# Two feed-forwards whose work is ordered by a planner or written out unit by unit, on one Trainium2 core

## The chip, the core and the metric

The kernel runs on one core of one Trainium2 chip. A core has five engines that run beside each other, each with its own queue of instructions: TensorE (PE, matrix products into the accumulator memory PSUM), VectorE (DVE), ScalarE (ACT), GpSimd (POOL) and SyncE (SP, which here only issues transfers). PE's loads of the stationary operand are listed apart (PEld). Each engine takes its instructions in order; an instruction that needs another engine's result waits on a semaphore. The metric is the device time of one execution in microseconds, and the kernel before is timed as the median of three runs.

## What is computed

A block of two layers over 512 positions `x` and 256 context positions, width 1024, all in float32. Each layer has a mixer (attention and others, not touched here) and a gated feed-forward whose input is normalised, scaled and shifted by modulation vectors; the modulation comes from a matrix `ada_w` times a small vector. The part that matters:

```python
def swiglu(h, w_in, w_out):
    g, u = jnp.split(h @ w_in, 2, axis=-1)
    return (jax.nn.silu(g) * u) @ w_out

    # per layer l
    mod = silu_c @ ada_w[l] + ada_b[l]
    modc = silu_cc @ ada_w[l] + ada_b[l]
    ...
    h = h + g2 * swiglu(modulate(h, norm2_g[l], sh2, sc2), ffn_w_in[l], ffn_w_out[l])
    if need_ctx:                       # layer 0 alone
        hc = hc + cg2 * swiglu(modulate(hc, norm2_g[l], csh2, csc2), ffn_w_in[l], ffn_w_out[l])
```

The hidden width is 2816, that is 22 hidden tiles of 128. Layer 0 works on 768 columns (positions and context), layer 1 on 512.

## The kernel before

**Products in three matmuls.** Every float32 operand is split in a high and a low part (`hi`, a rounded copy; `lo`, the rest). A product takes three matmuls per 128 rows: hi·hi, hi·lo, lo·hi (`mm3`, lines 100 to 102 of the profile). So each weight needs a cast on ScalarE (`slot`, line 913) and a subtraction on GpSimd or VectorE (line 917) before TensorE can use it.

**Seven products per hidden tile.** For hidden tiles 2 or 3 and up, the input product of a hidden tile is done by a scheme of seven half-size products instead of eight (`product`, numbered 1 to 7). Each has four steps of 128 rows: 12 matmuls of 384 columns in layer 0, of 256 in layer 1. The weights of products 1, 2 and 4 are quarters of the raw weight tile (`raw`, 1 MB, line 804); those of 5, 6, 3 and 7 are sums or differences that VectorE makes (line 968), all in one tile per hidden tile (`t` or `sq`). The results go to a wide PSUM tile of two banks, `pw`: products 1, 6, 7, 4 add up in its first half (`ps0`), 5 and 3 in its second (`ps1`); product 2 has a PSUM tile of its own. Between the products the partial sums are read out:

- after 1: copy of 2 (996), add (997), SiLU (999); after 6: copy (1001); after 5: copy into `u` (1005)
- after 3: add (1008), SiLU (1010); after 7: add to `u` (1012), multiplication (1014); after 4: multiplication (1017)
- then the hidden tile is split into hi and lo (116, 117)

**Output units.** The output product of a pair of hidden tiles is spread over later hidden tiles: per hidden tile four units a, b, c, d (`s2`), each for 128 output rows: 6 matmuls of 512 columns and, in layer 0, 6 of 256 for the context, into PSUM tiles `pb` of which there are three. VectorE adds each to the residual (766). Their weights come in tiles of 512 KB (`rawo`, line 925).

**Modulation of layer 1.** During layer 0's feed-forward, 48 tiles of `ada_w` are loaded on SyncE's queue (216) into two buffers and reduced by VectorE (222, "dots"); the first 16 of them serve positions and context, two dots each.

**Who sets the order.** The program is written in the order of lines 1079 to 1094, one string per hidden tile ("2156ab37cd4" and so on). Outside of a few explicit edges (`issue_after`), a planner then orders each engine's instructions by readiness and written order on an estimated timeline; so what stands in the queues is a mix of two or three hidden tiles. Waits are set per tile of memory, PSUM tiles included.

The loops in question are those over hidden tiles 3 to 21 in `ffn(0)` and `ffn(1)`. Ahead of them stand the direct tiles (two in layer 0, three in layer 1) and, in layer 0, hidden tile 2.

Of the kernel before, what the change touches and what calls it, by code (L numbers as in the profile page):

```python
# [6 lines left out]
F32 = mybir.dt.float32  # L7
# [7 lines left out]
P = 128  # L15
# [11 lines left out]
class Builder:  # L27
# [191 lines left out]
    def ada_dot(self, l, j, k, t, who):  # L219
        junk = self.adap.tile([P, D], BF16, name=self.uid("junk"), tag="junk", bufs=1)  # L220
        col = l * 48 + j * KT + k
        self.nc.vector.scalar_tensor_tensor(junk, t, 1.0, self.cb[who], ALU.mult, ALU.mult,
                                            accum_out=self.acc[who][:, col:col + 1])

# [538 lines left out]
    def residual(self, l, j, m, off, n, ps):  # L763
        for who, c, r in self.cols(off, n):
            h = self.h(who, m)[:, c]
            self.nc.vector.scalar_tensor_tensor(h, ps[:, r], self.modcol(l, j, m, who), h, ALU.mult, ALU.add)  # L766

# [34 lines left out]
    def ffn_in(self, l, f, pool):  # L802
        t = pool.tile([P, 2048], F32, name=self.uid("raw"), tag="raw", bufs=1 if pool is not self.Rf else 2)
        self.nc.sync.dma_start(t, self.a["ffn_in"][l, f])
        return t
# [43 lines left out]
    def ffn(self, l):  # L849
# [7 lines left out]
        if both:  # L857

            for n, shape, bufs in (("rawo", [P, 1024], 1), ("hs", [P, T], 1), ("u", [P, NH], 1), ("w", [P, 1024], 5)):
# [4 lines left out]
        def ada_some(n):  # L864
            for _ in range(min(n, len(todo))):
                ll, j, k = todo.pop(0)
                t = self.ada_tile(ll, j, k)
                for who in range(2 if j < 2 else 1):
                    self.ada_dot(ll, j, k, t, who)
# [39 lines left out]

        def slot(src, t=None):  # L910
            t = wtile() if t is None else t
            with tc.issue_after(self.first_sq.ins) if (3, 8)[l] <= self.nslot < 12 else ExitStack():
                nc.scalar.copy(t[:, 0, :], src)  # L913
            self.nslot += 1
            sums_due = (8, 12)[l] < self.nslot <= (15, 21)[l]
            eng = nc.vector if sums_due or l == 1 and self.nslot % 4 == 0 else nc.gpsimd
            eng.tensor_tensor(t[:, 1, :], src, t[:, 0, :].bitcast(F32), ALU.subtract)  # L917
            return t
# [3 lines left out]

        def load(src, cols):
            t = ring.tile([P, cols], F32, name=self.uid("rawo"), tag="rawo", bufs=(1, 2)[l])
            nc.sync.dma_start(t, src)
            return t

# [42 lines left out]

        def more(n, f, ins):

            if todo and n in (1, 3, 6, 7) and f >= 4:
                with tc.issue_after(ins.ins):
                    ada_some(1)

        def product(n, f):
# [16 lines left out]
            if n == 1:  # L994
                g = st["g"] = self.gated_tile(ring if f % 3 == 2 else None)
                nc.scalar.copy(g[:, :NH], st["p2"])
                ins = nc.vector.tensor_tensor(g[:, :NH], g[:, :NH], ps0, ALU.add)
                more(1, f, ins)
                nc.scalar.activation(g[:, :NH], g[:, :NH], AF.Silu)
# [6 lines left out]
            elif n == 3:  # L1006
                g = st["g"]
                ins = nc.vector.tensor_tensor(g[:, NH:], g[:, NH:], ps1, ALU.add)  # L1008
                more(3, f, ins)
                nc.scalar.activation(g[:, NH:], g[:, NH:], AF.Silu)  # L1010
            elif n == 7:
                ins = nc.vector.tensor_tensor(st["u"], st["u"], ps0, ALU.add)  # L1012
                more(7, f, ins)
                nc.vector.tensor_tensor(st["g"][:, NH:], st["g"][:, NH:], st["u"], ALU.mult)
            elif n == 4:
# [9 lines left out]
                del state[f], raws[f], sums[f]  # L1025
                more(4, f, self.last_s1)

        def s2_part(fs, m, W, off, n):
            ps = self.bank()[:, :n]
            self.dense(ps, W, [(hi[:, off:off + n], lo[:, off:off + n]) for hi, lo in [hid[f] for f in fs]])  # L1030
            self.residual(l, 5, m, off, n, ps)

        def s2_weights(g, m):

            if m % 4 == 0:
                outs[g] = load(a["ffn_out"][l, g, :, 256 * m:256 * m + 1024], 1024)
                if g == NF // 2 - 1:
                    f = NF + m // 4
                    pool = ring if l and f % 3 == 2 else self.Rf
                    self.big = pool.tile([P, 2048], F32R, name=self.uid("raw"), tag="raw", bufs=1 if pool is ring else 2)  # L1040
            if m % 2 == 0:
                o = m % 4 * 512
                t = self.big[:, o:o + 1024].rearrange("p (a b) -> p a b", a=2) if g == NF // 2 - 1 else None
                w2[g] = slot(outs[g][:, m % 4 * 256:m % 4 * 256 + 512], t)
            w = w2[g]
            return [(w[:, 0, c:c + P], w[:, 1, c:c + P]) for c in range(m % 2 * 256, m % 2 * 256 + 256, P)]

        def s2(g, m):

            W = s2_weights(g, m)  # L1050
            for off, n in whos:
                s2_part((2 * g, 2 * g + 1), m, W, off, n)

        hid, outs, w2, Wl = [], {}, {}, []

# [16 lines left out]
        for v in ("5 6 22 12 52 62 32 7 72 4 h 42", "5 6 d 4 7 h")[l].split():  # L1072
            if v == "d":
                direct(2, 1)
            elif v == "h":
                for f in range(nd):
                    hide(f)
            elif len(v) == 1:
                quarter(int(v))
            else:  # L1080
                product(int(v[0]), int(v[1]))
        for f in range(3, NF):
            todo_m = [(0, m) for m in range(8)] if f == 3 else [(f // 2 - 1, f % 2 * 4 + m) for m in range(4)]
            for v in ("2156ab37cd4", "2a1b56c3d74", "2a1b56c3de7f4ghij", "2a1b56c3de7f4g")[f % 2 if f < NF - 1 else l + 2]:
                if v in "abcd":
                    for _ in range(2 if f == 3 else 1):
                        s2(*todo_m.pop(0))
                elif v.isdigit():
                    product(int(v), f)
                else:  # L1090
                    m = "efghijkl".index(v)
                    Wl.append(s2_weights(NF // 2 - 1, m))
                    for off, n in whos:
                        s2_part((NF - 2,), m, Wl[m][:1], off, n)
        ahead = len(Wl)
        for m in range(ahead, KT):
            Wl.append(s2_weights(NF // 2 - 1, m))
        sq = self.sumsq()
# [305 lines left out]
```

## Time and profile before

| | us |
|---|---|
| median of three runs | 1640.68 |
| lowest, highest | 1636.35, 1644.80 |
| profiled execution, first to last instruction | 1641.9 |
| PE busy | 1542.8 |
| DVE busy | 1073.0 |
| POOL busy | 766.9 |
| ACT busy | 724.5 |

The profiled execution's own time is its span. A line of the groups reads: line of the kernel, engine, operation, output tile <- input tiles, shapes, count; then busy time in us and the mean of one in ns; then the idle time of the engine just before them and who ended it. A line of the timeline reads: start, duration, engine, line, operation; in brackets the idle time before it and its releaser. TensorE's matmuls are pipelined, so the durations of neighbours overlap, and the distance between starts tells the rate. A line of the busy time by windows reads: window, its length, then busy time and count of PE, PEld, DVE, ACT, POOL, the granted clock, the share of DMA time and GB/s. A line of the waits reads: who waited for whom, us in total, times, the longest.

### The profile page before, as it was taken

To read this page: it belongs to the slowest core of one execution; us is meant where nothing else is said; L and a number is where in the kernel's file an instruction comes from. 1 tells how busy PE (TensorE), PEld (TensorE's weight loads), DVE (VectorE), ACT (ScalarE), POOL (GpSimd) and SP (SyncE) were. 2 spreads that over 40 slices of the span, in tenths; PEclk is the share of its full clock that TensorE was granted. 3 is DMA by queue.
4 is the path that set the end of the run, shared out by engine and by line. 5 is a ranking of instruction groups with operands and counts; after the bars stand their busy time and mean duration, and the time that the engine had idled before them with its cause. 6 is when DMAs were issued, how large, how long until landed. Compare 5 with 4: busy or idle time off the path is not lost.

```text
span 1641.9 us, 24642 instructions
## 1 busy us (share of the span) xinstructions
PE 1542.8 (94%) x9547; PEld 1367.1 (83%) x9547; DVE 1073.0 (65%) x1980; ACT 724.5 (44%) x1472; POOL 766.9 (47%) x543
## 2 busy tenths in 40 slices
PE   6999989999999999999999988999989999999996
PEld 4776877899899889998989978777868989898886
DVE  4621788756857788666665585665667857666665
ACT  2423675645533233333333244555664544444443
POOL 0463221062157666666666316532222466675662
PEclk9999989999999999999999999999999999999998
DMA  8744100141223343343432012110233222322201
GB/s 317 298 153 169 40 7 1 65 139 68 76 79 116 105 139 131 105 150 126 142 131 77 27 51 91 52 33 25 74 116 123 65 103 92 101 90 103 90 27 52
DMA packets 47957, 161.98 MB, mean 99 GB/s; under 512 B 5472, under 2 KB 9952, under 8 KB 40160
## 3 DMA queue, kind: packets, MB, share of 16 engines
q1 hardware_dynamic: 47696, 160.28, 28.4%
q8 instruction: 75, 1.23, 0.3%
q14 instruction: 42, 0.34, 0.1%
q10 hardware_dynamic: 144, 0.13, 0.0%
HBM read 158.29 MB, written 2.10 MB: 98 GB/s over the span
## 4 chain that ended last, share of the span: by engine, by line
PE 69%; DVE 11%; POOL 6%; DMA 5%; ACT 4%; issue 3%; POOLq 0%; SPq 0%; DVEq 0%; ACTq 0%
PE pw L100 9%; PE pw L101 9%; PE pw L102 9%; PE pb L100 7%; PE pb L101 7%; PE pb L102 7%; POOL w L917 5%; DMA raw<-ffn_in 3%; PE pf L100 3%; PE pf L101 2%; PE pf L102 2%; PE pb L1257 2%; PE pb L1246 2%; PE pf L351 2%; DVE t L968 2%
## 5 line engine op out<-in xcount | busy, mean ns | idle before, releaser
L100 PE MATMUL pw<-ax,w 128*128 128x384 f32 (+2 forms) x732 | 237.5, 328 | 16.1 <-DVE q L1012 6.7
L101 PE MATMUL pw<-ax,w 128*128 128x384 f32 (+2 forms) x732 | 237.9, 325 | 4.1 <-DVE ax L458 2.5
L78 POOL TENSOR_TENSOR w<-raw,w 128x512 fp32r<-128x512 f32 (+1 forms) x84 | 127.6, 1526 | 243.2 <-ACT w L75 220.8
L102 PE MATMUL pw<-ax,w 128*128 128x384 f32 (+2 forms) x732 | 236.7, 325 | 2.1 <-POOL w L917 2.1
L917 POOL TENSOR_TENSOR w<-raw,w 128x512 fp32r<-128x512 f32 x119 | 177.7, 1507 | 54.2 <-ACT w L913 53.4
L917 POOL TENSOR_TENSOR w<-t,w 128x512 fp32r<-128x512 f32 x90 | 133.4, 1482 | 139.9 <-ACT w L913 136.5
L100 PE MATMUL pb<-hh,w 128*128 128x512 f32 x480 | 167.3, 362 | 12.8 <-ACT hh L116 8.3
L766 DVE SCALAR_TENSOR_TENSOR xT<-pb,mod,xT 128x512 f32<-128x512 f32 (+3 forms) x208 | 144.5, 704 | 43.8 <-PE pb L102 43.1
L101 PE MATMUL pb<-hh,w 128*128 128x512 f32 x480 | 171.2, 358 | 0.5 <-POOL hh L117 0.5
L102 PE MATMUL pb<-hh,w 128*128 128x512 f32 x480 | 170.7, 357 | 0.0
L100 PEld LDWEIGHTS pw<-ax,w 128*128 128x128 f32 x732 | 142.0, 195 | 27.2 <-DVE q L1012 8.1
L100 PE MATMUL pw<-T,w 128*128 128x384 f32 (+1 forms) x508 | 159.1, 314 | 4.8 <-DVE hs L1008 2.4
L101 PE MATMUL pw<-T,w 128*128 128x384 f32 (+1 forms) x508 | 158.6, 312 | 4.0 <-DVE T L117 4.0
L102 PE MATMUL pw<-T,w 128*128 128x384 f32 (+1 forms) x508 | 158.2, 312 | 0.0
L101 PEld LDWEIGHTS pw<-ax,w 128*128 128x128 f32 x732 | 142.6, 195 | 12.1 <-DVE ax L458 3.4
L102 PEld LDWEIGHTS pw<-ax,w 128*128 128x128 f32 x732 | 142.4, 195 | 6.0 <-POOL w L917 2.7
L913 ACT CAST w<-t 128x512 fp32r<-128x512 f32 x104 | 64.5, 621 | 176.8 <-DVE t L968 122.5
L917 POOL TENSOR_TENSOR w<-rawo,w 128x512 fp32r<-128x512 f32 x63 | 94.1, 1493 | 66.5 <-ACT w L913 66.5
L100 PEld LDWEIGHTS pb<-hh,w 128*128 128x128 f32 x480 | 89.5, 189 | 27.0 <-ACT hh L116 10.8
L100 PEld LDWEIGHTS pw<-T,w 128*128 128x128 f32 x508 | 97.2, 192 | 9.7 <-DVE hs L1008 3.9
L101 PEld LDWEIGHTS pw<-T,w 128*128 128x128 f32 x508 | 97.4, 192 | 6.6 <-DVE T L117 4.6
L102 PEld LDWEIGHTS pb<-hh,w 128*128 128x128 f32 x480 | 90.3, 188 | 13.1
(363 smaller groups left out, 4056.7 us busy)
## 6 DMA issues: line engine op xcount, KB each, us to landing
raw<-ffn_in SPq DMA_DIRECT2D x44, 1024.0 KB, 4.9
ar<-ada SPq DMA_DIRECT2D x24, 1024.0 KB, 7.3
ar<-ada SPq DMA_DIRECT2D x48, 512.0 KB, 3.5
rawo<-ffn_out SPq DMA_DIRECT2D x44, 512.0 KB, 3.9
raw<-odd_out SPq DMA_DIRECT2D x32, 256.0 KB, 2.7
raw<-qk SPq DMA_DIRECT2D x16, 256.0 KB, 7.9
raw<-uv SPq DMA_DIRECT2D x16, 256.0 KB, 2.7
raw<-even_out SPq DMA_DIRECT2D x8, 512.0 KB, 4.2
```

Of the source, the lines that this page charges most:

```text
L78: eng.tensor_tensor(lo, raw, hi.bitcast(F32), ALU.subtract)
L100: mm(out, s[0], m[0], start=start, stop=False, **kw)
L101: mm(out, s[0], m[1], start=False, stop=False, **kw)
L102: return mm(out, s[1], m[0], start=False, stop=stop, **kw)
L351: nc.tensor.matmul(ps[32 * q:32 * q + 32, :w], cst[:, k, :], t[:, w * q:w * q + w], start=k == 0, stop=k == KT - 1, skip_group_check=True)
L766: self.nc.vector.scalar_tensor_tensor(h, ps[:, r], self.modcol(l, j, m, who), h, ALU.mult, ALU.add)
L913: nc.scalar.copy(t[:, 0, :], src)
L917: eng.tensor_tensor(t[:, 1, :], src, t[:, 0, :].bitcast(F32), ALU.subtract)
L968: nc.vector.tensor_tensor(t, x, y, how)
L1246: last = nc.tensor.transpose(pt[:, x * P:(x + 1) * P], es[2 * (x % 2) + x // 2][:, kb * P:(kb + 1) * P], self.ident)
L1257: nc.tensor.matmul(po[64 * h:64 * h + 64, :], V[vb][:, 64 * g:64 * g + 64], t[:, h * TC:h * TC + TC], start=kb == 0, stop=kb == nb - 1, sk ...
```

## The change

It rewrites the loop over hidden tiles 3 to 21 of both feed-forwards.

- `run(key, ...)` issues an instruction after the last one that went through `run` with the same engine key, so that PE, DVE, ACT, POOL and SP each keep the written order within the loop.
- The loop is flattened into units: products and output units, per hidden tile 2 1 5 a 6 b 3 7 c d 4 for all of them.
- A second list, `jobs`, holds the weight preparations (sum where there is one, cast, low part) in the order of their use. Before the loop `R` jobs are issued, 8 in layer 0 and 12 in layer 1, and then one after each product and each pair of output units.
- Sums go to tiles of their own, three in turn, instead of one tile per hidden tile. Low parts go to GpSimd, in layer 1 those of output weights to VectorE.
- Output weights are loaded in half tiles (256 KB), two buffers in layer 0 and six in layer 1. Raw weights are loaded two or three hidden tiles ahead.
- Modulation tiles are loaded on ScalarE's queue, after 2, after 5 and after an output unit c, and reduced after 1, 3 and 4: three per hidden tile instead of four.
- Product 2 goes to the PSUM tile `pf` instead of one of the three `pb`.

```diff
+        def run(key, fn, *args, **kw):
+
+            with tc.issue_after(tail[key].ins) if key in tail else ExitStack():
+                tail[key] = fn(*args, **kw)
+            return tail[key]
...
+        def ada_load():
+            if todo:
...
+                run("ACT", nc.scalar.dma_start, t, a["ada1"][r:r + P, :])
+                tiles.append((ll, j, k, t))
...
+        nrawo = (2, 6)[l]
+        halves = [(g, h) for g in range(NF // 2) for h in range(4)]
+
+        def load():
+            if halves:
+                g, h = halves.pop(0)
+                t = ring.tile([P, 512], F32, name=self.uid("rawo"), tag="rawo", bufs=nrawo)
+                run("SP", nc.sync.dma_start, t, a["ffn_out"][l, g, :, h * 512:h * 512 + 512])
+                outs.append(t)
...
-            for v in ("2156ab37cd4", "2a1b56c3d74", "2a1b56c3de7f4ghij", "2a1b56c3de7f4g")[f % 2 if f < NF - 1 else l + 2]:
+            for v in "215a6b37cd4" if f < NF - 1 else ("215a6b37cdef4ghij", "215a6b37cdef4g")[l]:
...
+        R = (8, 12)[l]
...
+        def sum_tile():
+            self.ns += 1
+            sumt.append(self.sumsq()[:, :512] if self.ns % 3 == 2 else self.tmp("t"))
+            return sumt[-1]
...
+        def job():
...
+            if j[0] == "s":
+                Wt[j] = slot(outs.pop(0), None, ("POOL", "DVE")[l])
+                load()
...
+                    add("DVE", src, x, y, how)
+                Wt[j] = slot(src, None, "POOL")
...
+        def unit(n, f):
...
+            for j in range(4):
+                c = slice(j * P, (j + 1) * P)
+                run("PE", self.mm3, out, (w[:, 0, c], w[:, 1, c]), op[n][j], j == 0 and n in (1, 2, 5), j == 3)
...
+            if n == 2:
+                run("ACT", nc.scalar.copy, A, out)
+                ada_load()
+            elif n == 1:
+                add("DVE", A, A, ps0, ALU.add)
+                run("ACT", nc.scalar.activation, A, A, AF.Silu)
+                ada_dots()
+            elif n == 6:
+                run("ACT", nc.scalar.copy, B, ps0)
+            elif n == 5:
...
+                run("ACT", nc.scalar.copy, st["u"], ps1)
+                ada_load()
+            elif n == 3:
+                add("DVE", B, B, ps1, ALU.add)
+                run("ACT", nc.scalar.activation, B, B, AF.Silu)
+                ada_dots()
+            elif n == 7:
+                add("DVE", st["u"], st["u"], ps0, ALU.add)
+                add("DVE", B, B, st["u"], ALU.mult)
...
+        for _ in range(R):
+            job()
+        for u in units:
+            if u[0] == "s":
+                g, m = u[1:]
+                for off, n in whos:
+                    s2_part((2 * g, 2 * g + 1), m, pieces(Wt[("s", g, m // 2 * 2)], m), off, n, True)
+                if m % 4 == 2:
+                    ada_load()
+                if m % 2 == 0:
+                    continue
...
+            else:
+                unit(*u)
+            job()
```

More of the change, by code (lines that the diff above doesn't have):

```diff
@@ L1025, in product, with s2_part, pieces @@
                 del state[f], raws[f], sums[f]
-                more(4, f, self.last_s1)
-        def s2_part(fs, m, W, off, n):
+        def s2_part(fs, m, W, off, n, chain=False):
             ps = self.bank()[:, :n]
[L1030 to L1045, printed above, removed]
-            return [(w[:, 0, c:c + P], w[:, 1, c:c + P]) for c in range(m % 2 * 256, m % 2 * 256 + 256, P)]
[L1048 to L1054, printed above, removed]
+            A = [(hi[:, off:off + n], lo[:, off:off + n]) for hi, lo in [hid[f] for f in fs]]
+            if not chain:
+                self.dense(ps, W, A)
+                self.residual(l, 5, m, off, n, ps)
+                return
+            for k in range(len(W)):
+                run("PE", self.mm3, ps, W[k], A[k], k == 0, k == len(W) - 1)
+            run("DVE", self.residual, l, 5, m, off, n, ps)
+        def pieces(w, m):
+            return [(w[:, 0, c:c + P], w[:, 1, c:c + P]) for c in range(m % 2 * 256, m % 2 * 256 + 256, P)]
+        hid, outs = [], []
         nd = (2, 3)[l]
@@ L1086, in ffn @@
                     for _ in range(2 if f == 3 else 1):
[L1087 to L1097 removed]
+                        g, m = todo_m.pop(0)
@@ L1098, in ffn @@
+        ahead = sum(u[0] == "t" for u in units)
+        while jobs:
+            job()
         sq = self.sumsq()
```

121 lines of the change are left out of this document (98 added, 23 removed).

## The prediction

> **What bounds the kernel now.** I read the page's first part, then the busy time of the two feed-forward loops by windows, then single instructions in the timeline, then the lists of waits and the groups by shape.
>
> ```profile
> span 1641.9 us, 24642 instructions
> ...
> PE 1542.8 (94%) x9547; PEld 1367.1 (83%) x9547; DVE 1073.0 (65%) x1980; ACT 724.5 (44%) x1472; POOL 766.9 (47%) x543
> ```
>
> TensorE is busy 94% of the span. Busy is not full rate, so I take the rate from start times. First the loop of layer 0 (hidden tiles 3 to 21), then the same loop of layer 1:
>
> ```profile
> 470.00:930.00 460.00, 444.10 (x2486) 416.41 (x2485) 315.61 (x459) 156.57 (x282) 297.37 (x191) 0.99 0.34 115
> 1310.00:1610.00 300.00, 286.29 (x1929) 263.54 (x1927) 190.90 (x271) 126.95 (x262) 191.13 (x136) 0.99 0.25 85
> ```
>
> ```profile
> 663.08 0.33 PE L100 MATMUL pw<-ax,w 128*128 128x384 f32 x1
> ...
> 665.51 0.33 PE L102 MATMUL pw<-T,w 128*128 128x384 f32 x1
> ...
> 665.88 0.56 DVE L1012 TENSOR_TENSOR q<-q,pw 128x384 f32<-128x384 f32 x1 [0.47 <-PE pw L102]
> ...
> 666.39 0.39 PE L100 MATMUL pb<-hh,w 128*128 128x512 f32 x1
> ...
> 667.80 0.28 PE L100 MATMUL pb<-hh,w 128*128 128x256 f32 x1
> ...
> 668.39 0.28 PE L102 MATMUL pb<-hh,w 128*128 128x256 f32 x1
> ```
>
> ```profile
> 1608.68 0.28 PE L100 MATMUL pw<-ax,w 128*128 128x256 f32 x1
> ...
> 1609.64 0.28 PE L102 MATMUL pw<-ax,w 128*128 128x256 f32 x1
> 1610.03 0.42 DVE L1008 TENSOR_TENSOR hs<-hs,pw 128x256 f32<-128x256 f32 x1 [0.78 <-PE pw L102]
> ...
> 1610.50 0.39 PE L100 MATMUL pw<-T,w 128*128 128x256 f32 x1 [0.58 <-DVE hs L1008]
> 1610.73 0.28 PE L101 MATMUL pw<-T,w 128*128 128x256 f32 x1
> ```
>
> Undisturbed, a matmul of 384 columns follows the last after 0.174 us (14 steps from 663.08 to 665.51), of 512 after 0.235 (six from 666.39), of 256 after 0.12. A hidden tile of layer 0 has 84, 24 and 24 of them: 23.05 us, 0.175 each; one of layer 1 has 84 of 256 and 24 of 512: 15.7 us, 0.146 each. So the 2486 and 1929 matmuls of the windows need 434 and 281 us, and lose 26 and 19. **The change can win at most about 45 us in the loops**: the order that the planner found already overlaps two hidden tiles and is within 6% of TensorE's rate. The losses hang on late weights:
>
> ```profile
> PE pb L100 <- ACT hh L116: 8.3, 6, 2.9
> ...
> DVE t L968 <- DMA raw<-ffn_in: 19.2, 8, 5.2
> ...
> SPq L216 <- DVE junk L222: 246.9, 45, 15.0
> ```
>
> SyncE's queue stands 246.9 us behind the two modulation buffers, so raw weights come late, VectorE's sums wait 19.2 us for them, and TensorE waits at the end of that chain.
>
> **The change, part by part.**
>
> Weights 8 or 12 tiles ahead, sums in three tiles in turn, output weights in 256 KB halves, modulation loads on ScalarE's queue: these remove that chain. Raw weights are asked for two or three hidden tiles ahead, a half tile two tiles of work before its use, and 8 tiles are some 20 us. So I credit all 45 us. The halves cost 44 more issues on SyncE, and 48 issues move to ScalarE, which is busy 156.57 of 460 us; if their cover goes, one half tile costs its landing:
>
> ```profile
> raw<-odd_out SPq DMA_DIRECT2D x32, 256.0 KB, 2.7
> ```
>
> ```profile
> L917 POOL TENSOR_TENSOR w<-raw,w 128x512 fp32r<-128x512 f32 x55 | 86.1, 1573 | 15.7 <-ACT w L913 14.9 <-DVE t L968 0.8
> ...
> L117 POOL TENSOR_TENSOR hh<-hs,hh 128x768 fp32r<-128x768 f32 x19 | 36.4, 1917 | 5.3 <-ACT hh L116 5.1
> ```
>
> All low parts of layer 0 go to GpSimd (9 per tile of 1.57 us and one of 1.92: 16 of at least 23 us) and cost nothing while it stays below TensorE's time. A modulation load on ScalarE waits for the dot two loads back (two buffers); behind it stand the cast of a weight 8 tiles ahead and an activation that waits for VectorE anyway: 0, or one dot of 1.54 us if that cover goes. VectorE and ScalarE get 129 and 119 more semaphore instructions; they are short and lie in the queues walked through below.
>
> The written order of TensorE is the part that costs. Each hidden tile is 2 1 5 a 6 b 3 7 c d 4, chained. Products 1, 6, 7, 4 fill one half of a wide PSUM tile and 5, 3 the other, but the program waits for the tile, not the half: in the row at 1610.50 product 7 (first half) waits for VectorE's add of product 3 (second half). In the new order product 5 stands right behind 1 and 7 right behind 3, with nothing between, and the compiled program has exactly these waits. Before, the planner put other work there, and few such waits show (layer 1: us in total, times, longest):
>
> ```profile
> PE pw L100 <- DVE hs L1008: 1.8, 3, 0.8
> ```
>
> I call each place a join. Its least price: in layer 1, 1609.64 to 1610.50 is 0.86 us instead of 0.12, and the second matmul comes 0.11 late: 0.85. In layer 0, VectorE starts 0.37 after the last matmul's start (665.51 to 665.88) and takes 0.56; with the same rest that is 0.37 + 0.56 + 0.05 − 0.17 + 0.11 = 0.92. Two joins, 19 tiles, two layers: 19 × 2 × (0.92 + 0.85) = 67 us. **Joins alone eat the 45 and 22 more.**
>
> VectorE's order is chained too, so an add behind a join waits for whatever was written before it. Layer 1:
>
> ```profile
> L766 DVE SCALAR_TENSOR_TENSOR xT<-pb,mod,xT 128x512 f32<-128x512 f32 x69 | 50.3, 742 | 1.0 <-PE pb L102 0.9
> L968 DVE TENSOR_TENSOR t<-raw,t 128x512 f32<-128x512 f32 x11 | 17.3, 1569 | 3.2 <-POOL w L917 3.2
> L917 DVE TENSOR_TENSOR w<-rawo,w 128x512 fp32r<-128x512 f32 x12 | 15.8, 1320 | 4.1 <-ACT w L913 3.8
> L968 DVE TENSOR_TENSOR t<-raw 128x512 f32<-128x512 f32 x21 | 14.7, 699 | 35.7 <-DMA raw<-ffn_in 19.9 <-POOL w L917 15.8
> ```
>
> ```profile
> L913 ACT CAST w<-rawo 128x512 fp32r<-128x512 f32 x33 | 20.4, 620 | 0.0
> ...
> L996 ACT COPY hs<-pb 128x256 f32<-128x256 f32 x17 | 6.3, 370 | 2.7 <-PE pb L102 2.7
> ```
>
> ```profile
> L917 POOL TENSOR_TENSOR w<-raw,w 128x512 fp32r<-128x512 f32 x43 | 61.5, 1446 | 11.8 <-ACT w L913 11.8
> ...
> L117 POOL TENSOR_TENSOR hh<-hs,hh 128x512 fp32r<-128x512 f32 x18 | 28.7, 1595 | 0.4 <-ACT hh L116 0.3
> ```
>
> A product takes TensorE 1.43, an output unit 1.4. From the end of product 2 at 0: ScalarE has copied it out (0.37) at 0.95, since the cast of a sum stands ahead to 0.55, casts (0.62) an output half tile to 1.6, VectorE makes its low part (1.32) to 2.95, and only then adds product 1, to 3.35. Product 5 begins at 3.45; product 1 had ended at 1.43. Wait with the slow second matmul: 2.1. At the other join the residual of b (0.74) and another low part stand before the add of product 3: 5, a, 6 and b follow each other from 3.45 to 9.2, residual to 10.1, low part to 11.45, add to 11.9; product 3 ended at 10.6: 1.4. Together 3.5 us. A VectorE instruction of this size takes 0.70 where GpSimd leaves it alone (the row of t<-raw); with that for the low parts it is 1.55 + 0.85 = 2.4. Layer 1: 46 to 66 us.
>
> Layer 0, with modulation dots behind products 1, 3 and 4:
>
> ```profile
> L222 DVE SCALAR_TENSOR_TENSOR junk<-ar,cb 128x1024 bf16<-128x1024 f32 x64 | 98.6, 1541 | 0.2
> L766 DVE SCALAR_TENSOR_TENSOR xT<-pb,mod,xT 128x512 f32<-128x512 f32 x77 | 57.3, 744 | 20.2 <-PE pb L102 20.1
> ...
> L968 DVE TENSOR_TENSOR t<-raw,t 128x512 f32<-128x512 f32 x13 | 13.0, 1002 | 2.8 <-POOL w L917 2.8
> ...
> L968 DVE TENSOR_TENSOR t<-t,raw 128x512 f32<-128x512 f32 x12 | 8.2, 685 | 2.8 <-POOL w L917 2.7
> ...
> L1014 DVE TENSOR_TENSOR hs<-hs,q 128x384 f32<-128x384 f32 x12 | 16.9, 1406 | 0.0
> ```
>
> Both adds are prompt (0.92 each). But c and d need four PSUM banks of three, so d's second part waits for the residual of c's first. From the add of product 3 on, VectorE has a dot 1.54 to 1.62, a sum 1.0, product 7's add 0.55, the multiplication 1.4, a sum 0.7, the residual 0.74: 6.0 us, while TensorE gets there 5.75 us after that add (7, c, half of d). The wait is 0.45 with one dot and 2.1 with two (the first 16 of 48 tiles serve both streams: 5.3 hidden tiles). Sum: 13.7 × 2.3 + 5.3 × 3.9 = 52 us, at least 35.
>
> Loops: 35 + 46 − 45 = +36 to 52 + 66 − 45 = +73. I take +63, near the upper end: GpSimd's load stays as in the rows that have the longer times (7 × 1.45 + 1.6 of some 18.5 us, 63%; before 191.13 of 300). What happens ahead of the loops, where the first 8 or 12 tiles are now prepared beside the direct tiles, no row shows; I bound it by −10 to +15 us and take 0.
>
> The profiled execution took 1641.9 us, 1.2 over the median of the runs: 1641.9 + 63 = 1705.
>
> **Weighed against the skill.** One wait in the trace was followed by a slow clock:
>
> ```profile
> 1484.15 0.39 PE L100 MATMUL pw<-ax,w 128*128 128x256 f32 x1 [2.50 <-DVE q L1012]
> ...
> 1485.72 0.41 PE L102 MATMUL pw<-ax,w 128*128 128x256 f32 x1
> 1485.94 0.41 PE L100 MATMUL pw<-ax,w 128*128 128x256 f32 x1
> ...
> 1488.28 0.41 PE L102 MATMUL pw<-ax,w 128*128 128x256 f32 x1
> ```
>
> After 2.50 us idle the step became 0.215 us instead of 0.12 from about 1485.3 to 1488.5, 15 steps: 1.4 us lost. The Trainium skill ("TensorE: Matmul & The Clock Gate", HAM oscillation) asks only for no idle gaps over about 3.4 us; by it no join of 2.1 us costs clock and the sum stays 1705, while by the row it may. A second place: the Trainium skill ("PSUM — Partial Sum Buffer", PSUM bank collisions) says to guard PSUM by bank, and the two halves are different banks; by that rule the join need not exist, and the sum would be 1641.9 − 45. The wait at 1610.50 shows that this program guards the whole tile.
>
> **Rivals.** (1) Joins alone: VectorE is never late. For it: VectorE is free 35% of the time. Against: its order is fixed. 1641.9 + 22 = 1664. (2) Joins of 2.1 us also drop the clock, as at 1484.15: 19 × 1.4 = 27 on top, 1732. Against it: 2.1 is less than 2.5. (3) Faster: the joins are covered, and the removed weight chain decides. It turns at 45 / 76 joins = 0.59 us per join; below that the kernel gains, down to 1597. Against it: the two least prices are 0.85 and 0.92, and no matmul stands between. (4) Gain and joins cancel, within 0.5% (8 us; less than that a measurement here can hardly tell from no change).
>
> **How the numbers follow.** Forecast 1705: 0.60 (1680 to 1725). Rival 1: 0.17. Rival 2: 0.13. Rival 3: 0.07. Rival 4: 0.03. Range 1655 (rival 1 less 10 ahead of the loops) to 1740 (rival 2 and a little ahead of the loops): it leaves out rivals 3 and 4 and some of 2. Faster 0.07, same 0.03, slower 0.90.
>
> **What would show it.** TensorE waiting for VectorE's adds of products 1 and 3 some 19 times each per layer, 0.6 us or more each; per hidden tile 25 to 27 us in layer 0 and 18 to 19 in layer 1; layer 1's first join longer than the second; no wait of the loops left on raw weights or on GpSimd's low parts. Wrong if those waits are absent or under 0.6 us, if TensorE still waits for weights, or if the time moved ahead of the loops.

## The result, and the profile after

The changed kernel takes 1720.72 us (median of four runs, 1720.02 to 1721.14), the kernel before 1640.72: a ratio of 1.0489 with a 95% interval of 1.0469 to 1.0509. The change costs 80 us.

The page of the changed kernel, first its span and busy times, then, of TensorE's groups of matmuls, the one with most idle time ahead of it:

```profile
span 1718.5 us, 24909 instructions
...
PE 1564.2 (91%) x9547; PEld 1373.0 (80%) x9547; DVE 1056.4 (61%) x1969; ACT 733.7 (43%) x1472; POOL 762.1 (44%) x554
...
L100 PE MATMUL pw<-T,w 128*128 128x384 f32 (+1 forms) x508 | 169.5, 334 | 82.0 <-DVE hs L869 79.1
```

The same group before:

```profile
L100 PE MATMUL pw<-T,w 128*128 128x384 f32 (+1 forms) x508 | 159.1, 314 | 4.8 <-DVE hs L1008 2.4 <-ACT T L116 1.6 <-ACT u L1005 0.8
```

TensorE does the same 9547 matmuls, but stands idle for 82.0 us, before 4.8, just ahead of the `T` products (products 5, 6, 7 and 4, whose inputs are sums). The casts, low parts, sums, copies and adds of the loops now carry the line of `run`, 869. The list of TensorE's waits, for the whole span, for layer 0's loop (470 to 990 us) and for layer 1's (1310 to 1700):

```profile
PE pw L100 <- DVE hs L869: 79.1, 75, 8.7
```

```profile
PE pw L100 <- DVE hs L869: 29.6, 37, 1.4
PE pb L100 <- DVE xT L766: 3.9, 6, 1.1
```

```profile
PE pw L100 <- DVE hs L869: 49.4, 38, 8.7
```

There are 75 waits for VectorE's adds of products 1 and 3, 37 in layer 0 and 38 in layer 1: two per hidden tile. TensorE has no wait on weights, raw or prepared, in either window.

To see where the 76.6 us between the two profiled executions lie, I take the distance from each matmul's start to the next and subtract the undisturbed one of its size (0.173 us for 384 columns, 0.232 for 512, 0.119 for 256, 0.064 for 128, all read from stretches where nothing waits). What is left over is TensorE's loss, here by stage; a loop is counted from its first to its last matmul on a split hidden tile (`hh`), so the output units behind it are in it.

| loss against TensorE's rate, us | before | after |
|---|---|---|
| up to layer 0's first output unit | 63.3 | 65.2 |
| layer 0's loop | 30.5 | 50.7 |
| from there to layer 1's first output unit | 72.3 | 77.5 |
| layer 1's loop | 23.8 | 73.2 |
| behind it | 7.3 | 7.3 |

20 us are lost in layer 0's loop, 49 in layer 1's. One join of layer 1, product 1 to product 5, in the timeline of the changed kernel:

```profile
1516.82 1.27 POOL L869 TENSOR_TENSOR w<-t,w 128x512 fp32r<-128x512 f32 x1
...
1516.95 0.28 PE L102 MATMUL pw<-ax,w 128*128 128x256 f32 x1
1517.07 1.56 DVE L869 TENSOR_TENSOR w<-rawo,w 128x512 fp32r<-128x512 f32 x1 [1.53 <-ACT w L869]
1518.56 0.41 DVE L869 TENSOR_TENSOR hs<-hs,pw 128x256 f32<-128x256 f32 x1
...
1519.02 0.39 PE L100 MATMUL pw<-T,w 128*128 128x256 f32 x1 [1.79 <-DVE hs L869]
```

Product 1's last matmul starts at 1516.95, but VectorE first makes the low part of an output weight (1.56 us), then the add, and product 5 starts 2.07 us after the start of that matmul. Behind this join the clock held; behind 12 of the 17 of its length it did not (below). The other join of the same layer, product 3 to product 7:

```profile
1506.09 1.29 POOL L869 TENSOR_TENSOR w<-sq,w 128x512 fp32r<-128x512 f32 x1 [2.76 <-ACT w L869]
...
1507.18 0.75 DVE L869 TENSOR_TENSOR w<-rawo,w 128x512 fp32r<-128x512 f32 x1
...
1507.94 0.42 DVE L869 TENSOR_TENSOR hs<-hs,pw 128x256 f32<-128x256 f32 x1
...
1508.42 0.39 PE L100 MATMUL pw<-T,w 128*128 128x256 f32 x1 [0.52 <-DVE hs L869]
```

Here the same low part takes 0.75 us. An instruction of GpSimd lies beside it for its first 0.20 us; beside the low part of 1.56 us one lies for 1.02.

Below, the length of a join is the distance between the last matmul ahead of it and the first behind it, less the undisturbed distance. It is 1.05 and 0.88 us (means of the first and second join) in layer 0, where the first join is 1.50 in the first five tiles behind the first output unit and 0.88 in the other thirteen; in layer 1 it is 1.93 for the first (17 of 19 lie between 1.93 and 2.00; the very first, 8.85, stands ahead of the first output unit, and the last is 0.74) and 0.67 for the second.

### The profile page after: what moved, and what is told of

The parts are those of the page before. It is cut to its first block, busy times and chain, and to the rows that moved or that the text cites. A ratio compares the mean times of both kernels' runs of the same rounds, so it can differ in the third digit from the quotient of the medians.

```text
span 1718.5 us, 24909 instructions
## 1 busy us (share of the span) xinstructions
PE 1564.2 (91%) x9547; PEld 1373.0 (80%) x9547; DVE 1056.4 (61%) x1969; ACT 733.7 (43%) x1472; POOL 762.1 (44%) x554
## 5 line engine op out<-in xcount | busy, mean ns | idle before, releaser
L100 PE MATMUL pw<-T,w 128*128 128x384 f32 (+1 forms) x508 | 169.5, 334 | 82.0 <-DVE hs L869 79.1
L101 PE MATMUL pw<-ax,w 128*128 128x384 f32 (+2 forms) x732 | 235.3, 322 | 3.5 <-DVE ax L458 2.0
L100 PE MATMUL pw<-ax,w 128*128 128x384 f32 (+2 forms) x732 | 234.2, 323 | 2.7 <-ACT ax L194 1.6
L102 PE MATMUL pw<-ax,w 128*128 128x384 f32 (+2 forms) x732 | 234.1, 321 | 0.0
L869 POOL TENSOR_TENSOR w<-raw,w 128x512 fp32r<-128x512 f32 x114 | 172.9, 1528 | 80.1 <-ACT w L869 79.8
L100 PEld LDWEIGHTS pw<-T,w 128*128 128x128 f32 x508 | 99.5, 196 | 104.2 <-DVE hs L869 98.6
L100 PE MATMUL pb<-hh,w 128*128 128x512 f32 x480 | 177.6, 370 | 3.4 <-DVE xT L766 3.2
L101 PE MATMUL pb<-hh,w 128*128 128x512 f32 x480 | 176.3, 367 | 0.0
L102 PE MATMUL pb<-hh,w 128*128 128x512 f32 x480 | 176.0, 367 | 0.0
L101 PE MATMUL pw<-T,w 128*128 128x384 f32 (+1 forms) x508 | 161.0, 317 | 2.2 <-DVE T L117 2.2
L102 PE MATMUL pw<-T,w 128*128 128x384 f32 (+1 forms) x508 | 161.3, 318 | 0.0
L100 PE MATMUL pf<-ax,w 128*128 128x256 f32 (+2 forms) x420 | 140.5, 334 | 10.7 <-DVE qf L246 5.0
L101 PEld LDWEIGHTS pw<-ax,w 128*128 128x128 f32 x732 | 140.0, 191 | 10.8 <-DVE ax L195 2.9
L100 PEld LDWEIGHTS pw<-ax,w 128*128 128x128 f32 x732 | 139.8, 192 | 10.5 <-ACT ax L194 2.4
L102 PEld LDWEIGHTS pw<-ax,w 128*128 128x128 f32 x732 | 140.0, 191 | 2.7
L102 PE MATMUL pf<-ax,w 128*128 128x256 f32 (+2 forms) x420 | 139.2, 331 | 0.9 <-POOL w L869 0.9
L101 PE MATMUL pf<-ax,w 128*128 128x256 f32 (+2 forms) x420 | 139.3, 332 | 0.0
L869 DVE TENSOR_TENSOR hs<-hs,pw 128x384 f32<-128x384 f32 (+1 forms) x114 | 55.3, 485 | 94.6 <-PE pw L102 94.4
L100 PEld LDWEIGHTS pb<-hh,w 128*128 128x128 f32 x480 | 94.2, 196 | 19.4 <-DVE xT L766 6.9
```

The source lines that it names most:

```text
L100: mm(out, s[0], m[0], start=start, stop=False, **kw)
L101: mm(out, s[0], m[1], start=False, stop=False, **kw)
L102: return mm(out, s[1], m[0], start=False, stop=stop, **kw)
L869: tail[key] = fn(*args, **kw)
```

## The experiments

**The tile, not the data.** One line of `unit`: the two halves of a hidden tile's partial sums go to two PSUM tiles, of which each uses half.

```diff
-                st["w"] = [w_[:, :NH], w_[:, 512:512 + NH]]
+                st["w"] = [w_[:, :NH], self.wide()[:, :NH]]
```

> Only change to the kernel after: the two halves of the PSUM accumulator (products 1, 6, 7, 4 and products 5, 3) are two PSUM tiles instead of two halves of one, so product 5 no longer waits for the add of product 1, nor 7 for that of 3; all orders stay. Joins theory: the 36 + 47 us that TensorE loses at the 74 joins go, with the slow second matmuls (about 10) and most of the slow clock behind them (about 15); some of it comes back where VectorE is late elsewhere: 1635 us, 1615 to 1660. Rival, the written order as such or a busy VectorE is the bound and the joins are only where TensorE happens to wait: the waits move to the PSUM banks of the output units and to product 1, and the time stays within 15 us of 1720.

Measured: 1629.96 us, ratio 0.9938 (0.9917 to 0.9959). Not one of the 75 joins is left; layer 0's loop loses 23.9 us and layer 1's 4.3. So the joins, and the slow clock behind them, were worth 27 us in layer 0 and 69 in layer 1. Its list of waits shows what came out from behind them:

```profile
PE pb L100 <- DVE xT L766: 15.9, 18, 2.1
```

This is TensorE's second part of output unit d waiting for a PSUM bank. In the changed kernel it was 3.9 us in layer 0, since the joins had given VectorE time to catch up.

**Half of it.** The same edit for every other hidden tile (`if f % 2`), 10 of 19.

> As the kernel after, but only hidden tiles with an odd number (10 of the 19 in each loop) have two PSUM tiles. Joins theory: a price per join, so a little over half of the gain of two tiles everywhere: about 1675 us, 1660 to 1690. Rival, one common bound behind the joins: little or nothing until all are gone, above 1700.

Measured: 1667.24, ratio 1.0157 (1.0125 to 1.0189). 36 waits of 35.4 us are left. Layer 0's loop loses 37.0 (between 50.7 and 23.9), layer 1's 29.3 (between 73.2 and 4.3): the price is paid per tile, and in layer 1 over half of it goes with 10 of 19 tiles. Nine first joins of layer 1 are left, as long as in the changed kernel (1.93 to 2.00), and no slow clock follows any of them.

**VectorE's lateness.** Low parts of output weights go to GpSimd in layer 1 too.

```diff
-                Wt[j] = slot(outs.pop(0), None, ("POOL", "DVE")[l])
+                Wt[j] = slot(outs.pop(0), None, "POOL")
```

> As the kernel after, but in layer 1 the low parts of the output weights are made on GpSimd, not VectorE; the joins stay. If VectorE's written order makes the adds late (two low parts stand ahead of the adds of products 1 and 3): the joins of layer 1 fall from 1.26 us towards 0.75 us, about 15 to 19 us, and some slow clock with them: 1690 to 1705 us. If the joins alone are the price: 1720, within 5. If GpSimd becomes the bound (9 low parts of 1.45 us and one of 1.6 per hidden tile of 18 us): slower than 1720.

Measured: 1680.22, ratio 1.0244 (1.0204 to 1.0284), less than I expected. Both joins of layer 1 are now 0.74 us; its loop loses 35.0 us in place of 73.2. 37 joins of 0.74 and a slow second matmul (0.11) each make 31 of the 35. The first join became 1.19 us shorter, in 18 tiles 21 us of the 38; the rest is the clock, which no longer drops (below).

**Without the written order.** The chain in `run` is taken out, so that the planner orders the new program.

```diff
-            with tc.issue_after(tail[key].ins) if key in tail else ExitStack():
+            with ExitStack():
```

> As the kernel after, but no engine's order is chained: the planner orders the same instructions, with the weights 8 or 12 tiles ahead, half tiles, ScalarE's queue for modulation and one wide PSUM tile as before. One join is left instead of 74. Joins theory: 1640 us, 1615 to 1655, since the written order alone makes the joins. Rival, the other parts (half tiles, prefetch, ScalarE's queue) cost time too: above 1665.

Measured: 1640.88, ratio 1.0001 (0.9986 to 1.0017), with 6 waits of 8.4 us in place of 75 of 79.1. The other parts of the change (half tiles, sums in tiles of their own, loads on ScalarE's queue, the preparations written earlier) neither cost nor win anything in sum when the planner orders them: layer 0's loop loses 45.6 us, 15 more than before, layer 1's 16.7, 7 less, and the two stretches ahead of the loops 57.9 and 65.5, 12 less. VectorE has no wait on raw weights left in either loop, and yet the two loops together lose 8 us more than before.

**The bank wait.** As the two-tiles kernel, with the modulation dots behind product 3 moved behind product 6.

```diff
             elif n == 6:
                 run("ACT", nc.scalar.copy, B, ps0)
+                ada_dots()
...
                 run("ACT", nc.scalar.activation, B, B, AF.Silu)
-                ada_dots()
```

> The kernel of e1_two_tiles (each half of products in a PSUM tile of its own, 1630 us), with the modulation dots that stood behind product 3 moved behind product 6. In e1 the trace shows one wait left in layer 0's loop, TensorE's second part of output unit d for VectorE's residual, 15.9 us in 18 times. Theory (that wait is the lateness of VectorE, which has a dot of 1.54 us or two between the add of product 3 and the residual of c): it goes, and the time is 1630 - 16 to 18 = 1613 to 1617, layer 0's loop within 10 us of TensorE's rate. Rival (the dot is only late somewhere else, at product 3's add or at the sums): 1625 to 1632, with a new wait of TensorE on VectorE.

Measured: 1612.67, ratio 0.9843 (0.9815 to 0.9871). The wait falls to

```profile
PE pb L100 <- DVE xT L766: 5.2, 7, 0.9
```

and layer 0's loop loses 10.9 us (one over the 10 that I had allowed). Moving the dots behind one product, of 1.54 us and more each, by two units of TensorE's work is worth 17 us, 13 of them in this loop.

**The lead.** The two-tiles kernel with 3 weights ahead in place of 8 and 12.

```diff
-        R = (8, 12)[l]
+        R = (3, 3)[l]
```

> The kernel of e1_two_tiles with weights prepared 3 jobs ahead in both layers in place of 8 and 12. Theory (the written order removes the late weights, and a lead of 3 units, some 4.3 us of TensorE's work in layer 1 and 6.5 in layer 0, is longer than a sum, a cast and a low part, 0.7 + 0.6 + 1.6 = 2.9 us): 1625 to 1638, no wait of TensorE on low parts of more than a few us. Rival (the lead of 8 and 12 is what removed the late weights): TensorE waits for GpSimd's low parts, 1645 or more.

Measured: 1681.77, ratio 1.0267 (1.0245 to 1.0289): my theory fell, the rival held.

```profile
PE pw L102 <- POOL w L869: 35.5, 65, 0.7
PE pw L100 <- ACT w L869: 14.7, 17, 1.7
```

There are 65 waits of 0.55 us each for a low part, and 17 for a cast, 50 us in all. The loops lose 62.8 and 32.4 us in place of 23.9 and 4.3, which is 67 more; between the loops 12 us less are lost, and the difference in time is 52. I had counted three units of TensorE's work as the lead. But in the chained order a preparation stands behind the read-out of the unit that it follows, so it starts when that unit ends; only two units, 2.9 us in layer 1, are left for 2.9 us of work and its queueing, and in layer 0 dots stand ahead of the sums. This account is read from the order and the timeline; no run tests it by itself. The run does show that the written order needs a lead of more than 3.

**The price of a join, by dose.** Three kernels, all with the low parts on GpSimd as above, and 1, 2 or 3 more VectorE operations of 256 columns (0.45 us each; what they write is overwritten later) ahead of the add of product 1 in layer 1.

```diff
             elif n == 1:
+                for _ in range(1 if l else 0):
+                    add("DVE", B, A, ps0, ALU.add)
                 add("DVE", A, A, ps0, ALU.add)
```

> The kernel of e3_lows_on_gpsimd (1680 us; both joins of layer 1 at 0.74 us, no slow clock), with one more VectorE operation of 256 columns (some 0.42 us; its output is overwritten later) ahead of the add of product 1 in layer 1. Theory (a join costs its length, one for one, as long as the clock stays): first join 1.16 us, 17 to 18 times 0.42 = 7.5 us more, 1686 to 1690, no slow clock. Rival A (TensorE makes it up elsewhere): within 3 us of 1680. Rival B (a gap of 1.2 us is already enough for a slow clock): 1700 or more.

> As e7_one_op_late and e8_three_ops_late (first join of layer 1 at 1.20 us without and 2.11 us with a slow clock), with two operations more: the first join becomes 1.20 + 0.45 = 1.65 us. If the slow clock begins between 1.2 and 1.65: 17 to 19 x 0.45 = 8 us plus most of 23 us over e7, 1715 to 1723. If it begins between 1.65 and 2.1: 1700 +- 3. If its onset is gradual: a part of the tiles are slow, in between.

> As e7_one_op_late, with three such operations, so that the first join of layer 1 is 0.74 + 1.26 = 2.0 us, as long as in the changed kernel (1.93), though nothing else of the changed kernel's lateness is there. Theory (length alone: 18 x 1.26 = 23 us, no slow clock): 1703. Rival (a gap of about 2 us is followed by matmuls at half rate, some 1.5 us each in most tiles, as in the trace of the changed kernel): 1715 to 1730.

| operations more | time, us | first join | layer 1's loop loses | tiles with a slow clock |
|---|---|---|---|---|
| 0 | 1680.22 | 0.74 | 35.0 | 0 of 18 |
| 1 | 1691.92 | 1.20 | 43.1 | 0 of 18 |
| 2 | 1697.46 | 1.65 | 51.0 | 0 of 18 |
| 3 | 1728.43 | 2.11 | 82.1 | 15 of 18 |
| changed kernel | 1720.72 | 1.93 | 73.2 | 12 of 17 |

The 18 are the joins behind the first output unit. Up to 1.65 us a join costs its length, one for one: each operation adds 8 us to the loop, 18 × 0.45 by the count. The third adds 31: the same 8, and 23 more. So for one operation the theory held in the loop, though the time came out 2 us above its range; two fell in the branch of 1700 ± 3, without a slow clock; with three the rival held. (The ratios to the kernel before: 1.0325, from 1.0295 to 1.0355, for one; 1.0355, from 1.0328 to 1.0382, for two; 1.0548, from 1.0516 to 1.0579, for three.) The busy time of the window from 1330 to 1580 us, for one, two and three operations (window, length, busy time and count of PE, PEld, DVE, ACT, POOL, granted clock, DMA share, GB/s):

```profile
1330.00:1580.00 250.00, 227.33 (x1514) 206.29 (x1514) 144.37 (x198) 105.68 (x210) 179.62 (x140) 1.00 0.27 89
```

```profile
1330.00:1580.00 250.00, 221.53 (x1478) 201.12 (x1478) 133.60 (x207) 103.90 (x204) 176.00 (x138) 1.00 0.27 88
```

```profile
1330.00:1580.00 250.00, 219.63 (x1363) 198.75 (x1362) 114.86 (x200) 95.58 (x188) 160.50 (x126) 0.93 0.24 82
```

The second operation costs 36 matmuls in this window, the third 115, with the clock at 0.93. One such join in the timeline of the kernel with three:

```profile
1422.20 0.39 PE L100 MATMUL pw<-T,w 128*128 128x256 f32 x1 [1.95 <-DVE hs L869]
1422.42 0.28 PE L101 MATMUL pw<-T,w 128*128 128x256 f32 x1
1422.54 0.28 PE L102 MATMUL pw<-T,w 128*128 128x256 f32 x1
...
1423.02 0.42 PE L102 MATMUL pw<-T,w 128*128 128x256 f32 x1
1423.23 0.41 PE L100 MATMUL pw<-T,w 128*128 128x256 f32 x1
1423.44 0.41 PE L101 MATMUL pw<-T,w 128*128 128x256 f32 x1
```

Behind 1.95 us idle the distance between matmuls is 0.12 at first and 0.21 from about 0.6 us on.

Which of the long joins are spared can be read from the granted clock. In all these traces it falls to half for stretches of 3.41 us, sometimes several in a row, and within a trace these stretches start whole multiples of 3.41 us apart. Call each such piece of time a beat. Three beats of the changed kernel, the first around the join from 1418.72 to 1420.66:

```profile
1418.27:1421.68 3.41, 1.63 (x14) 1.43 (x13) 2.84 (x4) 1.24 (x3) 1.46 (x2) 1.00 0.05 17
1421.68:1425.09 3.41, 3.41 (x12) 2.90 (x11) 0.33 (x1) 1.13 (x3) 2.56 (x2) 0.50 0.22 65
1425.09:1428.50 3.41, 3.41 (x24) 3.09 (x23) 1.68 (x3) 1.22 (x3) 0.76 (x1) 1.00 0.00 0
```

Take the 62 first joins of layer 1 in the changed kernel (17), with half of the tiles (9), with two (18) and with three operations more (18), and cut each where a beat ends. A slow beat followed all 26 that had 1.91 us or more within one beat, none of the 34 that had at most 1.80, and one of two at 1.85. So a join of 1.65 could not bring it on, and one of 1.93 did only where nearly all of it lay within one beat. This is read from the traces; no run moved a join against the beat.

**Units between.** The changed kernel with one PSUM tile again, and another order of TensorE's units.

```diff
-            for v in "215a6b37cd4" if f < NF - 1 else ("215a6b37cdef4ghij", "215a6b37cdef4g")[l]:
+            for v in "21a5b63c7d4" if f < NF - 1 else ("21a5b63c7def4ghij", "21a5b63c7def4g")[l]:
```

> The changed kernel with one edit: TensorE's order in both loops is 2 1 a 5 b 6 3 c 7 d 4 in place of 2 1 5 a 6 b 3 7 c d 4, so that an output unit lies between 1 and 5, 5 and 6, 3 and 7, 7 and 4; the PSUM tile is one again, as in the changed kernel. Only 6 to 3 is bare, where the wait is for ScalarE's copy. Theory (a join costs only what no other work covers, an output unit is 1.4 us in layer 1 and 2.2 in layer 0): 38 joins of 0.7 to 0.9 = 27 to 34 us are left of the 82, no slow clock, and d's wait for a bank goes since 7 lies between c and d; before 1640.7 + 30 - 39 (both loops' gain in e5_dots_after_6) = 1625 to 1645. Rival (VectorE and ScalarE run later than an output unit is long, so the joins stay open): 1670 or more.

Measured: 1653.16, ratio 1.0087 (1.0067 to 1.0107).

```profile
PE pw L100 <- ACT hs L869: 20.1, 38, 1.0
PE pb L100 <- DVE xT L766: 9.9, 9, 4.6
PE pw L100 <- DVE hs L869: 9.7, 6, 3.4
```

The output units cover the joins on VectorE almost fully (6 waits are left of 75), and the one bare place, 6 to 3, costs its 38 waits, 26.3 us by starts, near the 27 counted. The time is 8 us above the range. Layer 0's loop has waits that I had not counted, by starts seven for an add (7.4 us), seven for a bank (6.1) and at its start one of 4.7 for a bank: I had not walked VectorE's queue, with its dots, through this order. Of the 80 us lost, this order alone wins back 68, with no more memory.

**The kernel before with two tiles.** The planner's own order, with only the tile edit above, in `product`.

> The kernel before, with one edit: each half of the products' results in a PSUM tile of its own, as in e1_two_tiles, the planner's order else free. Theory (in the kernel before the planner puts other work between the products, its waits for these adds are 4.8 us in all, and it is bound by late weights): 1632 to 1644, no difference from 1640.7 beyond 0.5%. Rival (the shared tile also holds the kernel before back, since the planner orders around it): 1625 or less, and then part of the 0.9843 of e5_dots_after_6 isn't due to the written order.

Measured: 1614.12, ratio 0.9848 (0.9828 to 0.9868): the rival held, and this is the run that changed my reading most. With one line the kernel before gains what all of the rewriting and two repairs gained. Its loops lose 15.4 and 10.6 us in place of 30.5 and 23.8. Where I had put these losses down to late raw weights, the waits inside layer 0's loop (470 to 930 us before, 470 to 940 here) say otherwise. Before:

```profile
DVE hs L1008 <- PE pw L102: 39.7, 10, 7.7
```

With two tiles, VectorE's waits there, and SyncE's queue over the whole span:

```profile
DVE t L968 <- DMA raw<-ffn_in: 25.3, 10, 4.0
...
DVE hs L1008 <- PE pw L102: 15.7, 9, 7.8
```

```profile
SPq L216 <- DVE junk L222: 232.9, 42, 13.6
```

In layer 0 VectorE waits for raw weights no shorter than before (25.3 us; it was 19.2), SyncE's queue stands behind the modulation buffers nearly as long (232.9; it was 246.9), and TensorE is faster all the same. What shrank is VectorE's wait for TensorE ahead of the add of product 3. The planner writes another order for this program, so these runs don't tell how much is the wait itself and how much the freer order.

In layer 1 late weights did cost TensorE time. Before, four of VectorE's waits on a raw weight (5.1 to 5.3 us) hold up the add of product 7 behind them, and TensorE waits for that add. One of the four, then TensorE's waits around layer 1's loop (1300 to 1620 us):

```profile
1483.07 0.69 DVE L968 TENSOR_TENSOR sq<-raw 128x512 f32<-128x512 f32 x1 [5.29 <-DMA raw<-ffn_in]
1483.68 0.42 DVE L1012 TENSOR_TENSOR q<-q,pw 128x256 f32<-128x256 f32 x1
```

```profile
PE pw L100 <- DVE q L1012: 6.7, 4, 2.5
PE pw L100 <- DVE u L1012: 4.7, 2, 2.4
```

With two tiles (1280 to 1590 us):

```profile
PE pw L100 <- DVE hs L1017: 5.0, 4, 2.2
PE pw L100 <- DVE u L1012: 0.3, 1, 0.3
```

By starts these four places cost TensorE 10.4 us before, and a slow beat follows two of them. With two tiles VectorE still waits there (3.8 to 4.9 us each), but TensorE loses 5.7 us, and a slow beat follows one.

**Both repairs.** The two-tiles kernel with the dots behind 6, hidden tile 2 of layer 0 in two tiles as well, and a lead of 8 in layer 1.

> The kernel of e5_dots_after_6 (1612.7) with hidden tile 2 of layer 0 too given a PSUM tile for each half, and weights prepared 8 jobs ahead in layer 1 as in layer 0, in place of 12. It asks whether the written order is worth anything beyond own tiles, since the planner's order with own tiles (e11_before_two_tiles) takes 1614.1: its loops lose 15.4 and 10.6 us against TensorE's rate, those of e5 10.9 and 4.3, but e5 loses 12 us more ahead of layer 0's loop (71.0 against 58.6). Theory (4 to 6 us of these 12 are hidden tile 2's joins and go; with fewer weights prepared ahead, VectorE reads out the direct tiles of layer 1 sooner, where one wait is 8.5 us, 0 to 8 less; the loops stay): 1600 to 1609. Rival A (the waits ahead of the loops are filled by others): 1610 to 1615. Rival B (a lead of 8 is too short in layer 1, as 3 was in both): its loop loses 5 to 15 us more, 1615 to 1625.

Measured: 1609.39, ratio 0.9815 (0.9801 to 0.9830), the fastest of all. The time is 0.4 us above the expected range. Ahead of layer 0's loop 5.3 us less are lost (65.7), as expected; between the loops 72.2 in place of 73.5, and layer 1's loop 6.4 in place of 4.3. Against the planner's order with the same tiles the written order loses 8 us less in the loops (11.3 and 6.4) and 7 more ahead of layer 0's. The two ratios differ by 0.3%, less than a measurement here can tell: beyond the tiles, no gain of the written order is shown.

## Why the prediction was right, and where not

The direction and the time (1705, measured 1720.7) came out because the main step held: two joins per tile, each at least a drained pipeline plus an add. By its terms, in us (the measured ones as differences of the losses by stage):

| term | predicted | measured | from |
|---|---|---|---|
| removed losses of the loops | −45 | −39 | loops of before less those with two tiles and dots behind 6 |
| joins and lateness, layer 0 | +35 to 52 | +40 | 50.7 − 10.9 |
| the same, layer 1, without a slow clock | +46 to 66 | +51 | 73.2 − 4.3 − 18 |
| slow clock, layer 1 | 0 (rival 2: +27) | +18 | 12 tiles, 1.5 each |
| elsewhere | 0 (−10 to +15) | +7 | 1.9 + 5.2 |
| sum | +63 | +77 | profiled executions |

That the sum came so near is in part luck. The upper ends of the terms add up to +73, and I took +63. Against those ends the joins and lateness of the two layers came out 27 us lower (12 and 15), while the slow clock, the credit and the stretches ahead of the loops came out 31 higher (18, 6 and 7), and this nearly cancels. That the joins are the main cost is not luck: two tiles take away all 75 of them, and 91 us.

- **Joins.** 76 foretold, 75 seen; in layer 0 1.05 and 0.88 us against 0.92 each with the slow second matmul (0.11) counted in, so 0.3 us more per tile than foretold. "Both adds are prompt" failed in the first five tiles, where the first join is 1.50: in the one at 504.87 the add stands behind two dots of 1.68 and 2.74 us.
- **Layer 1, first join.** 2.1 foretold, 1.93 + 0.11 measured, by the walk that was written: cast, low part beside GpSimd, add. The low part took 1.56 us in place of 1.32, but began as product 1 ended, 0.17 earlier than in the walk.
- **Layer 1, second join.** 1.4 foretold, 0.67 + 0.11 measured. The failed step is "with that for the low parts it is 1.55 + 0.85", from which I chose the long end: I took 1.32 us for every low part from GpSimd's mean load, while in a fixed order nearly every tile repeats the same neighbours, with 1.53 to 1.56 at the first join and 0.75 at the second. The low end, 0.85, was right.
- **Layer 0, bank wait.** 17 us foretold (13.7 × 0.45 + 5.3 × 2.1), 3.9 measured in 6 waits. The joins are longer than counted, and each gives VectorE time to catch up; with them gone the wait is 15.9, near the number.
- **The slow clock** was rival 2, and I argued against it with "2.1 is less than 2.5". That was the step that failed: a case that was seen sets no threshold. Nor was the wait at 1484.15 the only one of its kind: of four such waits in layer 1's loop before (2.5 to 2.7 us by starts), a slow beat followed two, at 1352.2 and 1485.3, and two, with at most 1.89 us of idle time in one beat, were spared. Rival 2 came true in 12 of 17 tiles, 18 us, which is more than the 14 by which the sum of 63 fell short of 77. Rival 1 (joins alone, 1664) is out: VectorE was late, and removing only that left 1680.
- **The credit of 45** was nearly right in size (39) and only partly right in cause. It was counted in windows that leave out the ends of the loops; over the whole loops before, 54 us are lost. "The losses hang on late weights" was read from waits on DMA and on SyncE's queue. It holds for some 13 us of layer 1: four waits behind a raw weight (10.4 us) and two slow beats (1.4 each). But with two tiles in the kernel before, VectorE's waits on raw weights stay and 28 of the 54 us go, 15 of them in layer 0. The same PSUM tile that makes the joins had held the kernel before back. I took three short waits of TensorE (1.8 us) for the tile's whole price there; in layer 1 the waits behind the add of product 7 shrank too. Through which of its waits the tile cost 15 us in layer 0 stays open.
- Per hidden tile, 25 to 27 us were foretold for layer 0 and 18 to 19 for layer 1; 23.05 + 50.7 / 19 = 25.7, and in layer 1 18.5 us from one first join to the next where the clock holds and 20.0 where it drops.

**Two rules beside these runs.** On the clock, the runs show full rate behind joins of 1.65 us and half rate behind most of 1.93 and 2.11. The Trainium skill ("TensorE: Matmul & The Clock Gate", HAM oscillation) asks for no idle gaps over about 3.4 us; measured here, 1.79 to 1.95 us idle was enough where 1.85 us or more of the join lay in one beat, so the measurement decides. On VectorE, the low part of one shape took 0.75 and 1.56 us. A GpSimd subtraction that had begun earlier lay beside them for 0.20 and 1.02 us, so that each took 0.54 to 0.55 us more than that. The add with one operand in PSUM stayed at 0.41 to 0.42, with a GpSimd subtraction beside it (most in the kernel with low parts on GpSimd) or without. The Trainium skill ("SBUF — State Buffer", Who interferes with whom) says that a VectorE instruction with two SBUF inputs contends with a GpSimd instruction that reads SBUF, that one with at most one, outside of VectorE's two-port modes, doesn't, and that the order of issue decides who is blocked; the rows agree.

## What to carry to other kernels

Before writing out an order, list for every pair of neighbours which memory tile they share: a wait is set by the tile that the program tracks, so two accumulators in one PSUM tile serialise although their data is apart, and splitting them was worth more than the whole rewriting. When a wait looks like the cause, check that the time goes if it goes; of waits on late data of some 5 us, TensorE paid 2.5 each with one PSUM tile and 0.7 to 2.4 with two. In a fixed order every operation keeps its neighbours, so price it by the neighbours that it has, not by a mean, and count the lead of a preparation from the end of the unit that it stands behind.

## What the hardware showed

- An idle gap of TensorE of 1.79 us inside dense work was followed by half rate, at a loss of about 1.5 us, in 12 of 17 cases, one of 1.95 us in 15 of 18, and one of 1.49 us (joins of 1.65) in none of 18; the nine joins of 1.93 with half of the tiles were all spared. So one third operation of 0.45 us cost 31 us. The half rate comes in beats of 3.41 us, behind a beat in which 1.91 us or more of a join lay, and not behind one with at most 1.80.
- A lost microsecond can be lost behind another: removing the joins raised the bank wait of layer 0 from 3.9 to 15.9 us, and a lead of weights too short by 0.55 us at a time in 65 waits, and for 17 casts, cost 67 us over the two loops.
- With the sums and GpSimd's low parts side by side (low parts on GpSimd in layer 1), the sums of two raw quarters took 1.25 us on VectorE, against 0.76 in the changed kernel; it cost nothing there, since TensorE did not wait for them.
